# VectorE's order in a state space stage: tied to the source, with inputs and sums a step apart

## The chip, the core and the metric

One core of a Trainium2 chip runs a whole small network in one launch. The metric is the device time of that launch in microseconds. The engines are TensorE (PE, with its weight loads as PEld), VectorE (DVE), ScalarE (ACT), GpSimd (POOL) and SyncE (SP, which issues the DMAs). Each takes its instructions in the order in which they were queued; they meet through semaphores.

## The reference

Two blocks of two layers each work on 256 tokens of width 1024: projections, mixers, norms and MLPs, all in fp32. The change lies in the first mixer of the second block, `mixer_sb_ssm`. It projects the tokens to q, k, v and u, 512 wide each, and computes two things side by side.

Stick-breaking attention, 8 heads of 64: `z = q k / 8`; the weight of position s for query t is `sigmoid(z)` times the product of `1 - sigmoid(z)` over the positions after s and before t. So it needs log sums of `softplus(z)` along s, then an exponential, then the product with v.

A state space model, 32 groups of 64 complex states, 16 channels each: `x_t = a x_(t-1) + B u_t`, `y_t = Re(C x_t) + d u_t`, over the 256 tokens. After it come `y = gelu(y)`, a gate `y * sigmoid(y W + b)` (GLU) and the mixer's output projection.

## The kernel before, in words

All large matmuls run as three matmuls of split operands: a weight tile arrives by DMA (`raw`), ScalarE writes its rounded part (`hi`, L362), VectorE the rest (`lo`, L364), and TensorE forms hi*hi + hi*lo + lo*hi (`mm3`, L386 to L388). I call L362 and L364 a split. Weights come in a fixed sequence; a split is traced one or two units ahead of its use.

The work is traced by generators. The projections are the main line (`transposed`, `natural`), which yield every few matmuls; at each yield `step()` advances the side generators by one step each. A planner then orders the instructions of each engine: it goes through them by their place in the trace and its own estimates of time, and gives a tile its buffer from a pool of fixed size when the tile is first written. An instruction traced later can so be queued earlier. `behind(ins)` makes what is traced inside it follow `ins` on the same engine, without a semaphore.

`_ssm_run` is one side generator (from the u projection on), `side_attention` the other (from the first half of k and q on). The states fill 16 sets of 128 partitions, taken 4 at a time (q = 0 to 3) as tile k = 0 to 3. Tokens are taken in pairs, so that 128 steps of two tokens are left. For each k and q: two matmuls with K = 64 (L1883; in fp32 a matmul stands as two instructions in the trace) form the input in a PSUM bank, the row half depending on q % 2; VectorE rotates it by a phase (products with cos and sin, L1887 and L1888, sums L1889 and L1890, into `w`), and runs two scans along the steps (L1892, into `xs`). After four q the result is rotated back (L1902 to L1909, four products and two sums on 128x512), over `w`. `outputs` (L1850 to L1858) multiplies `w` by C on TensorE, one k later, and adds d*u on VectorE (L1860, into `yT`). A k has three steps: q = 0, 1; q = 2, 3; rotation.

The attention takes half a head pair per step s = 0 to 7: `stage_a` forms masked scores in a PSUM bank (L1323 to L1326), ScalarE makes |z|, exp, ln(1 + .) of them (L1329 to L1331), VectorE the softplus (L1332); `stage_b`, a step later, adds the triangular sums to the same bank (L1337 to L1341) and ScalarE takes the exponential (L1344); `stage_c` multiplies by v (L1352), whose tile `vn` ScalarE copies from PSUM (L1394).

Pools that matter: `b4` has 7 buffers (uT, yT, qT, kT, vn, up, each k's w and xs, and the two row loads of the next norm, L1529), `b2` has 12 (the attention's tiles, the rotation's four), `b1` 7, and the PSUM pool `psw` 4 banks (inputs of a q, scores, outputs, stage c). After the side work come the rows of the output projection (`_rows`), GELU (L1658 to L1663) and the GLU's matmuls.

Of the kernel before, what the change touches and what calls it, by code (L numbers as in the profile page):

```python
# [12 lines left out]
ALU = mybir.AluOpType  # L13
# [92 lines left out]
def _offsets():  # L106
    off, table = 0, {}
    for key, parts in _units().items():
        if key[0] == "up":
            nkt, ncol = sum(len(p[2]) for p in parts) // 128, len(parts[0][3])  # L110
        else:
            nkt, ncol = len(parts[0][2]) // 128, sum(len(p[3]) for p in parts)
        table[key] = (off, nkt, ncol)
        off += nkt * 128 * ncol
    return table, off
# [144 lines left out]
class _Env:  # L260
# [5 lines left out]
    def __init__(self, ctx, tc, ws):  # L266
        self.tc, self.nc, self.ws = tc, tc.nc, ws
        self.pools = {}
        self.ctx = ctx
        self.ps = {k: ctx.enter_context(tc.tile_pool(name="ps" + k, bufs=4, space=PSUM)) for k in "aw"}  # L270
        self.table, _ = _offsets()
        self.seq = _sequence()
        self.pos = {k: n for n, k in enumerate(self.seq)}
        self.raws, self.parts = {}, {}
        self.loaded = self.cut = 0
        self.n = 0
        self.side = []
        self.after = self.marks = ()
# [181 lines left out]
def _hilo(e, hi, lo, src):  # L460

    return (e.nc.scalar.activation(out=hi, in_=src, func=AF.Copy),
            e.nc.vector.tensor_tensor(out=lo, in0=src, in1=hi.bitcast(F32), op=ALU.subtract))


class _Act:
# [27 lines left out]
class _Norm(_Act):  # L494
# [8 lines left out]
    def slice(self, xT, c):  # L503
        self.add(xT[:, 2 * c:2 * c + 2], self.g[:, 2 * c:2 * c + 2])
        if c == 0:
            self.e.after = self.last
        self.square(xT, c)
# [48 lines left out]
def kernel(ctx: ExitStack, tc: tile.TileContext, x: bass.AP, p: bass.AP, prm1: bass.AP,  # L556
# [61 lines left out]
    for i in range(2):  # L618
# [44 lines left out]
        def load_emb(i=i):  # L663
            pt = e.t("b2", [128, 2, 256])
            nc.sync.dma_start(out=pt, in_=p[i])
            emb.extend(e.t("b2", [128, 2, 256], F32R) for _ in range(2))
            _hilo(e, *emb, pt)
# [53 lines left out]
        norm = nxt  # L721
        dump(f"xp{i}", xT)
    _second(e, K, xT, norm, ssm, ln, out, dump)


# [562 lines left out]
def _second(e, K, xT, act, S, ln, out, dump):  # L1288
    nc, tc = e.nc, e.tc
    V, A, G, PE = nc.vector, nc.scalar, nc.gpsimd, nc.tensor  # L1290
    P, C, ident, negones = S["P"], S["C"], K["ident"], K["negones"]
# [6 lines left out]
    uT = e.t("b4", [128, 4, 256])  # L1298
    for c in range(2):
        e.run(e.transposed(("su", c), act,  # L1300
                           lambda b, bank, c=c: A.activation(out=uT[:, 2 * c:2 * c + 2], in_=bank, func=AF.Copy)))
    e.drain_all()
    yT = e.t("b4", [128, 4, 256])
    run = _ssm_run(e, P, C, S, uT, yT)
    e.add(run)

    qT = e.t("b4", [128, 4, 256])
# [8 lines left out]
    sc, ws = {}, {}  # L1316

    def stage_a(s):
        j, g = s // 2, s % 2
        hs = slice(64 * g, 64 * g + 64)  # L1320
        ps = e.bank()
        diag = ps[:, :].rearrange("p (a q) -> p a q", a=4)[:, 0:4:2]
        PE.matmul(out=diag, lhsT=im[:, 0], rhs=smask2, start=True, stop=False, skip_group_check=True)  # L1323
        PE.matmul(out=ps[:, 0:256], lhsT=kT[hs, j, 0:128], rhs=qT[hs, j, :], start=False, stop=False,
                  skip_group_check=True)
        PE.matmul(out=ps[:, 256:384], lhsT=kT[hs, j, 128:256], rhs=qT[hs, j, 128:256], start=False, stop=False,  # L1326
                  skip_group_check=True)
        l = e.t("b2", [128, 384])
        A.activation(out=l, in_=ps[:, :384], func=AF.Abs)  # L1329
        A.activation(out=l, in_=l, func=AF.Exp, scale=-1.0)  # L1330
        A.activation(out=l, in_=l, func=AF.Ln, bias=1.0)  # L1331
        V.scalar_tensor_tensor(out=l, in0=ps[:, :384], scalar=0.0, in1=l, op0=ALU.max, op1=ALU.add)  # L1332
        sc[s] = (ps, l)

    def stage_b(s):
        ps, sp = sc.pop(s)
# [24 lines left out]
    def side_attention():  # L1361
        ready, lag = [], 1
        for s in range(8 + lag):
            while s >= 4 and "qk" not in D:
                yield
            if s < 8:
                stage_a(s)
            if s >= lag:
                stage_b(s - lag)
                if (s - lag) % 2:  # L1370
                    ready.append((s - lag) // 2)
            yield
            if ready and "v" in D:
                stage_c(ready.pop(0))
        while ready:
            yield
            stage_c(ready.pop(0))
# [461 lines left out]
    S.update(cos=cosE, sin=sinE, m=m2, bT=bT, cexp=cexp, k0=k0)  # L1839


def _ssm_run(e, P, C, S, uT, yT):

    nc = e.nc
    V, A, G, PE = nc.vector, nc.scalar, nc.gpsimd, nc.tensor

    def outputs(k, w):
        u = uT[:, k].rearrange("p (j r) -> p r j", r=2)
        y = e.bank()[:, :256].rearrange("p (r j) -> p r j", r=2)
        PE.matmul(out=y[:, 0], lhsT=S["k0"][:, k], rhs=u[:, 0], start=True, stop=False, skip_group_check=True)  # L1850
        for v, r, c in ((0, 1, 0), (1, 1, 1), (2, 0, 0), (3, 0, 1)):
            for q in range(4):
                h = slice(32 * q, 32 * q + 32)
                if r == 1:
                    PE.matmul(out=y[h, 1], lhsT=S["cexp"][:, v, 4 * k + q], rhs=w[:, q, c], start=False, stop=False,
                              skip_group_check=True)
                else:
                    PE.matmul(out=y[h, 0, 1:128], lhsT=S["cexp"][:, v, 4 * k + q], rhs=w[:, q, c, 0:127],  # L1858
                              start=False, stop=v == 3, skip_group_check=True)
        V.scalar_tensor_tensor(out=yT[:, k].rearrange("p (j r) -> p r j", r=2), in0=u, scalar=P["d"][:, k:k + 1],  # L1860
                               in1=y, op0=ALU.mult, op1=ALU.add)


    up = e.t("b4", [128, 4, 2, 128])
    for q in range(4):
        for r in range(2):
            o = 64 * (q % 2) + 32 * r
            src = uT[32 * q:32 * q + 32].rearrange("p k (j r) -> p r k j", r=2)[:, r]
            if r:
                G.tensor_copy(out=up[o:o + 32, :, q // 2], in_=src)  # L1870
            else:
                A.activation(out=up[o:o + 32, :, q // 2], in_=src, func=AF.Copy)
    yield
    prev = None
    for k in range(4):
        w = e.t("b4", [128, 4, 2, 128])
        xs = e.t("b4", [128, 4, 2, 128])
        s = slice(4 * k, 4 * k + 4)
        for q in range(4):
            h = slice(64 * (q % 2), 64 * (q % 2) + 64)  # L1880
            ps = e.bank()[:, :256].rearrange("p (c j) -> p c j", c=2)
            for c in range(2):
                PE.matmul(out=ps[:, c], lhsT=S["bT"][h, c, 2 * k + q // 2], rhs=up[h, k, q // 2])  # L1883
            st = 4 * k + q
            tc_ = e.t("b1", [128, 2, 128])
            ts_ = e.t("b1", [128, 2, 128])
            V.tensor_tensor(out=tc_, in0=ps, in1=S["cos"][:, st].unsqueeze(1).to_broadcast([128, 2, 128]), op=ALU.mult)  # L1887
            V.tensor_tensor(out=ts_, in0=ps, in1=S["sin"][:, st].unsqueeze(1).to_broadcast([128, 2, 128]), op=ALU.mult)  # L1888
            V.tensor_tensor(out=w[:, q, 0], in0=tc_[:, 0], in1=ts_[:, 1], op=ALU.add)  # L1889
            V.tensor_tensor(out=w[:, q, 1], in0=tc_[:, 1], in1=ts_[:, 0], op=ALU.subtract)  # L1890
            for c in range(2):
                V.tensor_tensor_scan(out=xs[:, q, c], data0=S["m"][:, st:st + 1].to_broadcast([128, 128]), data1=w[:, q, c], initial=0.0,  # L1892
                                     op0=ALU.mult, op1=ALU.add)
            if q % 2:
                yield
        if prev is not None:
            outputs(*prev)
        cosb = S["cos"][:, s]
        sinb = S["sin"][:, s]
        ta = e.t("b2", [128, 4, 128])  # L1900
        tb = e.t("b2", [128, 4, 128])
        V.tensor_tensor(out=ta, in0=xs[:, :, 0], in1=cosb, op=ALU.mult)  # L1902
        V.tensor_tensor(out=tb, in0=xs[:, :, 1], in1=sinb, op=ALU.mult)
        V.tensor_tensor(out=w[:, :, 0], in0=ta, in1=tb, op=ALU.subtract)
        tc2 = e.t("b2", [128, 4, 128])
        td = e.t("b2", [128, 4, 128])
        V.tensor_tensor(out=tc2, in0=xs[:, :, 1], in1=cosb, op=ALU.mult)
        V.tensor_tensor(out=td, in0=xs[:, :, 0], in1=sinb, op=ALU.mult)
        V.tensor_tensor(out=w[:, :, 1], in0=tc2, in1=td, op=ALU.add)  # L1909
        prev = (k, w)  # L1910
        yield
    outputs(*prev)
# [181 lines left out]
```

## Time and profile before

| | us |
|---|---|
| median of 3 runs (range) | 1472.47 (1470.43 to 1473.62) |
| the profiled execution | 1469.84 |
| its span | 1468.1 |
| TensorE, VectorE, ScalarE busy in the span | 1446.8, 1077.4, 779.8 |
| TensorE's mean granted clock, share of full speed | 0.993 |

A row of the timeline gives the start in us from the span's start, the length, the engine, the line, the operation, the tile written and the tiles read, and in brackets how long the engine stood idle before it and what ended that. Neighbouring rows can overlap: an engine starts an instruction before the last one has ended. A line of the list of waits reads: who waited, for whom, us in total, times, the longest. Busy time counts matmuls whose ends are modelled. [...]

### The profile page before, as it was taken

The numbers are of one execution on the slowest core, as the hardware profiler recorded it, in microseconds if no ns is written. First come the engines' busy times: TensorE is split into PE (matmuls) and PEld (weight loads), VectorE is DVE, ScalarE is ACT, GpSimd is POOL, SyncE is SP. The second block draws the span as 40 slices with busy tenths as digits, with TensorE's granted clock in tenths as the row PEclk, the third lists the DMA queues.
The fourth block names the chain that finished last, engine by engine and source line by source line (L and its number), as shares of the span: only waits on it lengthen the run. The fifth ranks groups of instructions, "written<-read, shape, count | busy, mean of one in ns | idle before, by whom it ended". The sixth has DMA issues, their size and how long they took to land.

```text
span 1468.1 us, 24862 instructions
## 1 busy us (share of the span) xinstructions
PE 1446.8 (99%) x9740; PEld 1282.8 (87%) x9740; DVE 1077.4 (73%) x1857; ACT 779.8 (53%) x1248; POOL 202.4 (14%) x142
## 2 busy tenths in 40 slices
PE   9999999999999999999999999999999999999997
PEld 7878999999998779999999998778888798788886
DVE  6786668666678796679877778868666788686666
ACT  6665445444557564454654555455545456654442
POOL 2343313000033333203000200000000100100000
PEclk9999999999999999999999999899999999999999
DMA  8552445555545553555555454235555452265551
GB/s 294 189 188 99 171 172 175 198 187 186 180 154 189 197 174 131 175 174 176 187 199 180 158 178 152 78 129 194 194 190 182 151 193 103 100 214 189 187 191 68
DMA packets 70677, 250.59 MB, mean 171 GB/s; under 512 B 8096, under 2 KB 8480, under 8 KB 70560
## 3 DMA queue, kind: packets, MB, share of 16 engines
q1 hardware_dynamic: 70560, 249.01, 49.6%
q8 instruction: 76, 1.25, 0.3%
q14 instruction: 41, 0.34, 0.1%
HBM read 247.93 MB, written 1.05 MB: 170 GB/s over the span
## 4 chain that ended last, share of the span: by engine, by line
PE 88%; DVE 6%; ACT 2%; DMA 2%; issue 1%; POOL 0%; DVEq 0%; SPq 0%; ACTq 0%; POOLq 0%
PE psa L386 16%; PE psa L387 16%; PE psa L388 16%; PE psw L436 15%; PE psw L438 8%; PE psw L386 3%; PE psw L387 3%; PE psw L388 3%; DMA raw<-in_ws_dram 2%; DVE lo L364 2%; PE psw L1076 1%; ACT hi L362 1%; PE psw L1883 1%; PE psw L2028 0%; PE psw L773 0%
## 5 line engine op out<-in xcount | busy, mean ns | idle before, releaser
L364 DVE TENSOR_TENSOR lo<-raw,hi 128x1024 fp32r<-128x1024 f32 (+1 forms) x416 | 515.3, 1245 | 224.7 <-ACT hi L362 223.4
L362 ACT ACTIVATE hi<-raw 128x1024 fp32r<-128x1024 f32 (+1 forms) x448 | 465.6, 1047 | 395.4 <-issue 153.7
L436 PE MATMUL psw<-act,hi 128*128 128x512 f32 x960 | 340.8, 397 | 0.0
L438 PE MATMUL psw<-act,lo 128*128 128x256 f32 x960 | 268.0, 281 | 0.0
L436 PEld LDWEIGHTS psw<-act,hi 128*128 128x128 f32 x960 | 179.9, 188 | 41.1
L438 PEld LDWEIGHTS psw<-act,lo 128*128 128x128 f32 x960 | 181.4, 189 | 1.7
L388 PE MATMUL psa<-b,lo 128*128 128x256 f32 x640 | 180.4, 283 | 0.0
L387 PE MATMUL psa<-b,hi 128*128 128x256 f32 x640 | 180.2, 283 | 0.0
L386 PE MATMUL psa<-b,hi 128*128 128x256 f32 x640 | 177.8, 283 | 0.0
L386 PE MATMUL psa<-act,hi 128*128 128x256 f32 x456 | 132.1, 291 | 0.0
L388 PE MATMUL psa<-act,lo 128*128 128x256 f32 x456 | 130.0, 286 | 0.8 <-DVE lo L364 0.8
L387 PE MATMUL psa<-act,hi 128*128 128x256 f32 x456 | 130.6, 287 | 0.0
L386 PE MATMUL psa<-hi,act 128*128 128x512 f32 (+2 forms) x320 | 122.7, 390 | 1.2 <-ACT act L481 0.4
L388 PEld LDWEIGHTS psa<-b,lo 128*128 128x128 f32 x640 | 122.0, 191 | 0.1
L387 PEld LDWEIGHTS psa<-b,hi 128*128 128x128 f32 x640 | 122.0, 191 | 0.0
L387 PE MATMUL psa<-lo,act 128*128 128x512 f32 (+2 forms) x320 | 121.1, 382 | 0.6 <-DVE lo L364 0.5
L386 PEld LDWEIGHTS psa<-b,hi 128*128 128x128 f32 x640 | 120.4, 190 | 1.2
L388 PE MATMUL psa<-hi,act 128*128 128x512 f32 (+2 forms) x320 | 116.8, 382 | 0.0
L386 PE MATMUL psa<-hi,b 128*128 128x512 f32 x256 | 99.6, 390 | 0.0
L387 PE MATMUL psa<-lo,b 128*128 128x512 f32 x256 | 99.6, 390 | 0.0
L364 POOL TENSOR_TENSOR lo<-raw,hi 128x1024 fp32r<-128x1024 f32 x32 | 77.5, 2423 | 157.1 <-ACT hi L362 140.0
L388 PE MATMUL psa<-hi,b 128*128 128x512 f32 x256 | 98.7, 389 | 0.0
(364 smaller groups left out, 2656.3 us busy)
## 6 DMA issues: line engine op xcount, KB each, us to landing
raw<-in_ws_dram SPq DMA_DIRECT2D x450, 512.0 KB, 4.0
b<-in_ln_dram SPq DMA_DIRECT2D x8, 512.0 KB, 4.9
raw<-in_ws_dram SPq DMA_DIRECT2D x8, 280.0 KB, 4.2
raw<-in_ws_dram SPq DMA_DIRECT2D x4, 264.0 KB, 2.5
b<-in_x_dram SPq DMA_DIRECT2D x4, 256.0 KB, 4.7
out_dram<-b SPq DMA_DIRECT2D x4, 256.0 KB, 2.0
cb<-in_cb_dram SPq DMA_DIRECT2D x1, 676.0 KB, 6.6
b<-in_p_dram SPq DMA_DIRECT2D x2, 256.0 KB, 5.6
```

What stands on the lines that cost most here:

```text
L362: self.nc.scalar.activation(out=hi, in_=w, func=AF.Copy)
L364: eng.tensor_tensor(out=lo, in0=w, in1=hi.bitcast(F32), op=ALU.subtract)
L386: mm(out=out, lhsT=lh, rhs=rh, start=start, stop=False, skip_group_check=shared)
L387: mm(out=out, lhsT=lh, rhs=rl, start=False, stop=False, skip_group_check=shared)
L388: self.mlast = mm(out=out, lhsT=ll, rhs=rh, start=False, stop=stop, skip_group_check=shared)
L436: mm(out=bank.rearrange("p (v t) -> p v t", v=2), lhsT=h[:, c], rhs=act[2][k], start=k == 0, stop=False, skip_group_check=True)
L438: mm(out=bank[:, :256], lhsT=l[:, c], rhs=act[0][k], start=False, stop=k == len(hi) - 1, skip_group_check=True)
L1076: PE.matmul(out=o[64 * gg:64 * gg + 64, q0:256], lhsT=kvn[:, kt, v0:v0 + 64], rhs=pts[s - 2 + 2 * gg][:, 256 * kt:256 * kt + 256 - q0], st ...
L1883: PE.matmul(out=ps[:, c], lhsT=S["bT"][h, c, 2 * k + q // 2], rhs=up[h, k, q // 2])
```

## The change

A class `_Chain` stands for VectorE in `_ssm_run` and for the softplus. Each instruction issued through it is put behind the one issued through it before, so that these instructions have the source's order on VectorE; others, the splits among them, may go between. The softplus moves out of `stage_a` to the start of the attention's next step. In `_ssm_run` a tile's eight input matmuls are issued together, one step ahead of VectorE's work on them, into two whole PSUM banks: bank n holds q = n and n + 2, which use the same half of the rows. VectorE then works on two q at once: products of 128x512 and sums of 128x256 in place of 128x256 and 128x128, with temporaries from `b2` in place of `b1`. The scans and the rotation keep their sizes. A k still has three steps: matmuls; products, sums and scans; outputs of the last k and rotation.

```diff
             e.nc.vector.tensor_tensor(out=lo, in0=src, in1=hi.bitcast(F32), op=ALU.subtract))
 
 
+class _Chain:
+
+
+    def __init__(self, e, engine):
+        self.e, self.engine, self.last = e, engine, ()
+
+    def __getattr__(self, name):
+        def call(**kw):
+            with self.e.behind(self.last):
+                ins = getattr(self.engine, name)(**kw)
+            self.last = (ins,)
+            return ins
+        return call
+
+
 class _Act:
 
 
@@ -1301,7 +1316,8 @@
                            lambda b, bank, c=c: A.activation(out=uT[:, 2 * c:2 * c + 2], in_=bank, func=AF.Copy)))
     e.drain_all()
     yT = e.t("b4", [128, 4, 256])
-    run = _ssm_run(e, P, C, S, uT, yT)
+    order = _Chain(e, V)
+    run = _ssm_run(e, P, C, S, uT, yT, order)
     e.add(run)
 
     qT = e.t("b4", [128, 4, 256])
@@ -1329,8 +1345,11 @@
         A.activation(out=l, in_=ps[:, :384], func=AF.Abs)
         A.activation(out=l, in_=l, func=AF.Exp, scale=-1.0)
         A.activation(out=l, in_=l, func=AF.Ln, bias=1.0)
-        V.scalar_tensor_tensor(out=l, in0=ps[:, :384], scalar=0.0, in1=l, op0=ALU.max, op1=ALU.add)
         sc[s] = (ps, l)
+
+    def softplus(s):
+        ps, l = sc[s]
+        order.scalar_tensor_tensor(out=l, in0=ps[:, :384], scalar=0.0, in1=l, op0=ALU.max, op1=ALU.add)
 
     def stage_b(s):
         ps, sp = sc.pop(s)
@@ -1363,6 +1382,8 @@
         for s in range(8 + lag):
             while s >= 4 and "qk" not in D:
                 yield
+            if s >= lag:
+                softplus(s - lag)
             if s < 8:
                 stage_a(s)
             if s >= lag:
@@ -1839,10 +1860,10 @@
     S.update(cos=cosE, sin=sinE, m=m2, bT=bT, cexp=cexp, k0=k0)
 
 
-def _ssm_run(e, P, C, S, uT, yT):
+def _ssm_run(e, P, C, S, uT, yT, V):
 
     nc = e.nc
-    V, A, G, PE = nc.vector, nc.scalar, nc.gpsimd, nc.tensor
+    A, G, PE = nc.scalar, nc.gpsimd, nc.tensor
 
     def outputs(k, w):
         u = uT[:, k].rearrange("p (j r) -> p r j", r=2)
@@ -1876,23 +1897,27 @@
         w = e.t("b4", [128, 4, 2, 128])
         xs = e.t("b4", [128, 4, 2, 128])
         s = slice(4 * k, 4 * k + 4)
-        for q in range(4):
-            h = slice(64 * (q % 2), 64 * (q % 2) + 64)
-            ps = e.bank()[:, :256].rearrange("p (c j) -> p c j", c=2)
+        pss = [e.bank().rearrange("p (a c j) -> p a c j", a=2, c=2) for _ in range(2)]
+        for a in range(2):
             for c in range(2):
-                PE.matmul(out=ps[:, c], lhsT=S["bT"][h, c, 2 * k + q // 2], rhs=up[h, k, q // 2])
-            st = 4 * k + q
-            tc_ = e.t("b1", [128, 2, 128])
-            ts_ = e.t("b1", [128, 2, 128])
-            V.tensor_tensor(out=tc_, in0=ps, in1=S["cos"][:, st].unsqueeze(1).to_broadcast([128, 2, 128]), op=ALU.mult)
-            V.tensor_tensor(out=ts_, in0=ps, in1=S["sin"][:, st].unsqueeze(1).to_broadcast([128, 2, 128]), op=ALU.mult)
-            V.tensor_tensor(out=w[:, q, 0], in0=tc_[:, 0], in1=ts_[:, 1], op=ALU.add)
-            V.tensor_tensor(out=w[:, q, 1], in0=tc_[:, 1], in1=ts_[:, 0], op=ALU.subtract)
-            for c in range(2):
-                V.tensor_tensor_scan(out=xs[:, q, c], data0=S["m"][:, st:st + 1].to_broadcast([128, 128]), data1=w[:, q, c], initial=0.0,
-                                     op0=ALU.mult, op1=ALU.add)
-            if q % 2:
-                yield
+                for n in range(2):
+                    h = slice(64 * n, 64 * n + 64)
+                    PE.matmul(out=pss[n][:, a, c], lhsT=S["bT"][h, c, 2 * k + a], rhs=up[h, k, a])
+        yield
+        for n in range(2):
+            st = slice(4 * k + n, 4 * k + n + 3, 2)
+            tc_ = e.t("b2", [128, 2, 2, 128])
+            ts_ = e.t("b2", [128, 2, 2, 128])
+            bc = lambda t: t[:, st].unsqueeze(2).to_broadcast([128, 2, 2, 128])
+            V.tensor_tensor(out=tc_, in0=pss[n], in1=bc(S["cos"]), op=ALU.mult)
+            V.tensor_tensor(out=ts_, in0=pss[n], in1=bc(S["sin"]), op=ALU.mult)
+            V.tensor_tensor(out=w[:, n::2, 0], in0=tc_[:, :, 0], in1=ts_[:, :, 1], op=ALU.add)
+            V.tensor_tensor(out=w[:, n::2, 1], in0=tc_[:, :, 1], in1=ts_[:, :, 0], op=ALU.subtract)
+            for q in (n, n + 2):
+                for c in range(2):
+                    V.tensor_tensor_scan(out=xs[:, q, c], data0=S["m"][:, 4 * k + q:4 * k + q + 1].to_broadcast([128, 128]),
+                                         data1=w[:, q, c], initial=0.0, op0=ALU.mult, op1=ALU.add)
+        yield
         if prev is not None:
             outputs(*prev)
         cosb = S["cos"][:, s]
```

## Rows read from the trace of the kernel before

**Rows 1.** The page, parts 1 and 4: busy engines, and the chain that ended last.
```profile
PE 1446.8 (99%) x9740; PEld 1282.8 (87%) x9740; DVE 1077.4 (73%) x1857; ACT 779.8 (53%) x1248; POOL 202.4 (14%) x142
...
PE 88%; DVE 6%; ACT 2%; DMA 2%; issue 1%; POOL 0%; DVEq 0%; SPq 0%; ACTq 0%; POOLq 0%
```

**Rows 2.** Windows: length, busy time (x instructions) of PE, PEld, DVE, ACT, POOL; PEclk; DMA.
```profile
887.10:952.60 65.50, 62.97 (x450) 52.81 (x450) 59.30 (x142) 28.70 (x48) 0.00 (x0) 0.92 0.31 105
935.30:949.20 13.90, 11.37 (x68) 9.13 (x68) 13.90 (x39) 6.33 (x13) 0.00 (x0) 0.63 0.11 38
938.90:948.00 9.10, 7.91 (x33) 6.20 (x35) 9.10 (x29) 4.22 (x10) 0.00 (x0) 0.50 0.15 51
```

**Rows 3.** Waits of TensorE, 886.4 to 968.5: us in total, times, longest.
```profile
PE psw L1883 <- DVE b L1860: 1.3, 1, 1.3
PE psw L1883 <- DVE b L1888: 1.2, 1, 1.2
```

**Rows 4.** Waits of VectorE, 887.1 to 952.6.
```profile
DVE b L1887 <- PE psw L1883: 2.5, 3, 1.8
DVE b L1332 <- ACT b L1331: 2.1, 1, 2.1
```

**Rows 5.** Timeline of TensorE at two runs of input matmuls: start, us, line, operation.
```profile
890.95 0.28 PE L388 MATMUL psa<-act,lo 128*128 128x256 f32 x1
891.07 0.28 PE L386 MATMUL psa<-act,hi 128*128 128x256 f32 x1
891.28 0.71 PE L1883 MATMUL psw<-b,b 64*128 64x128 f32 x4
...
892.14 0.28 PE L388 MATMUL psa<-act,lo 128*128 128x256 f32 x1
...
899.48 0.72 PE L1883 MATMUL psw<-b,b 64*128 64x128 f32 x8
```

**Rows 6.** Timeline of VectorE: starts of neighbouring products, sums and rotations.
```profile
890.22 0.42 DVE L1887 TENSOR_TENSOR b<-psw,b 128x256 f32<-128x256 f32 x1
890.55 0.41 DVE L1888 TENSOR_TENSOR b<-psw,b 128x256 f32<-128x256 f32 x1
...
903.10 0.68 DVE L1902 TENSOR_TENSOR b<-b,b 128x512 f32<-128x512 f32 x1
903.70 0.69 DVE L1903 TENSOR_TENSOR b<-b,b 128x512 f32<-128x512 f32 x1
...
929.97 0.41 DVE L1888 TENSOR_TENSOR b<-psw,b 128x256 f32<-128x256 f32 x1
930.41 0.29 DVE L1889 TENSOR_TENSOR b<-b,b 128x128 f32<-128x128 f32 x1
930.62 0.28 DVE L1890 TENSOR_TENSOR b<-b,b 128x128 f32<-128x128 f32 x1
```

**Rows 7.** Timeline of three engines: who waits for a buffer of b4.
```profile
920.65 0.29 DVE L1889 TENSOR_TENSOR b<-b,b 128x128 f32<-128x128 f32 x1
...
930.68 0.50 PE L1850 MATMUL psw<-b,b 128*128 128x128 f32 x2
...
932.44 0.62 PE L1858 MATMUL psw<-b,b 128*32 128x127 f32 x16
...
933.50 2.62 DVE L1892 TENSOR_TENSOR_SCAN b<-m,b 128x128 f32<-128x128 f32 x8
...
945.39 1.08 ACT L1394 ACTIVATE b<-psa 128x512 f32<-128x512 f32 x2 [1.30 <-PE psw L1326]
```

**Rows 8.** Timeline at the end of the stage: last rotation, outputs, GELU, GLU's matmuls.
```profile
951.95 0.68 DVE L1909 TENSOR_TENSOR b<-b,b 128x512 f32<-128x512 f32 x1
...
957.12 0.48 DVE L1860 SCALAR_TENSOR_TENSOR b<-b,prm,psw 128x256 f32<-128x256 f32 x1 [1.80 <-PE psw L1858]
...
965.58 1.23 DVE L463 TENSOR_TENSOR b<-b,b 128x1024 fp32r<-128x1024 f32 x1
...
968.49 0.41 PE L386 MATMUL psw<-b,hi 128*128 128x256 f32 x2
```

## The prediction, made before the change was run

> **What bounds the kernel now.** I read the page first: TensorE is busy for 99% of the span and makes up 88% of the chain that ended last, VectorE 6% [rows 1]. So a change of VectorE's order pays only where TensorE lost time to VectorE. I then cut the stage of the state space run into windows. Over 887.1 to 952.6 VectorE was busy for 59.30 of 65.50 us, so it idled 6.2. Over 935.3 to 949.2 TensorE idled 13.90 - 11.37 = 2.5 us, and from 938.9 to 948.0 its granted clock was 0.50, the lower of its two levels [rows 2]. TensorE's list of waits has just two, both for VectorE, 1.3 and 1.2 us, both ahead of L1883 [rows 3]. Those rows are the finding: from about 935 to 949 VectorE sets the pace, and before and after that TensorE runs without a gap. VectorE's own waits in the same stretch are 2.5 us for L1883's matmuls and 2.1 us for a softplus's ScalarE input [rows 4]; the remaining 1.6 us are short ones, mostly for weight splits.
>
> The stage ends like this: VectorE's last rotation is issued at 951.95 (0.68 us), the last outputs at 957.12, the GELU's last operand at 965.58 (1.23 us, so 966.8), and TensorE takes it up at 968.49 [rows 8]. Two things thus meet at 968.49: TensorE's filling work, without a gap since 949, and the GELU, ready 1.7 us before.
>
> **The change, part by part.** Input matmuls. There are 64 instructions before and after. Before, they came as 12 runs of 4 and 2 runs of 8. One run of 4 pushes the dense matmuls apart by 892.14 - 891.07 less two spacings of 0.12 (891.07 - 890.95): 0.83 us. A run of 8, on both halves of the rows, takes 0.72 us against 0.71 [rows 5]: the second half rides along. So before: 14 x 0.83 = 11.6 us. After, a tile has one run of 16, two such pairs back to back. No row shows a run of 16; between 0.83 (all rides along) and 0.83 + 0.65 I take 1.3, so 4 x 1.3 = 5.2 us, and TensorE has 6.4 us less to do.
>
> Fewer, longer VectorE instructions. The 32 products of 128x256 come 0.33 us apart (890.22 to 890.55); 128x512 comes 0.60 apart (903.10 to 903.70), read from SBUF, the nearest row. 16 x (0.66 - 0.60) = 1.0 us less; 0 if PSUM costs more at that size. The 32 sums of 128x128 come 0.21 apart (930.41 to 930.62) and become 16 of 128x256, which I price as the products' 0.33: 16 x (0.42 - 0.33) = 1.4. Together 0 to 2.4, taken as 2.0. The 32 scans stay as they are.
>
> [...]
>
> The tie to the source's order. It adds no semaphore, only an order on VectorE: each product, sum, scan, rotation, output and softplus behind the one traced before it. The splits (L364) stay free to go between. The price is that needing neighbours stand together: L1889 right behind the L1888 that it reads starts 930.41 - 929.97 = 0.44 us after it, not 0.33 [rows 6]. Four such pairs a tile (product to sum, twice; the rotation's two sums), so 16 x 0.11 = 1.8 us more, or 0 where a split falls between.
>
> Waits that go. A tile's matmuls are traced a step before its products, so VectorE's 2.5 us for L1883 should go. The softplus is traced a step behind its scores, so ScalarE's three passes lie beside a whole step of VectorE work, and the 2.1 us should go [rows 4]. That is 4.6 us. Both times a split or a scan that was ready stood behind the waiting instruction.
>
> A wait that comes. The pool b4 has 7 buffers. From tile 1 on uT, qT, kT, up, yT, w and xs hold all 7. The next tile's w takes the old xs once that is rotated, but its own xs has to wait for the old w, which the outputs read last. The trace shows it: tile 2's first sum is at 920.65, its scans only at 933.50, right behind L1858's outputs of tile 1 (932.44 + 0.62), the last reader of tile 1's w; and the value tile's copy (L1394) waited for L1326, the last reader of kT, until 945.39 [rows 7]. In the tied order tile 2's scans stand in the line: the softplus and the rotation stand behind them, and so does any split queued after them, for which TensorE's dense matmuls wait. The scans wait for the outputs of tile 1, and these for one of the 4 PSUM banks of their pool. That pool is freer than before (two banks a tile where four were taken). A bank comes free when the tile's first two products are read, 1.2 us into its VectorE work (2 x 0.60); the outputs took 2.4 us with a stage b between them (930.68 to 933.06), about 1.4 by estimate without; the scans are due at 2.0 (two products and two sums). So the stall is 0.6 to 1.6 us and some way on TensorE's queue, taken as 2.0. Tile 1 is spared, for one buffer is still free then, and tile 3, since up comes free once its matmuls are done. The bounds are 0 and 11 (rival B). The products' move from pool b1 to b2 I cost at nothing: a rotation needs two b2 buffers at a time in the source's order. No DMA is moved; the norm's two row loads on SP's queue wait for b4 too, and get it sooner.
>
> Sum for VectorE: -2.0 + 1.8 - 4.6 + 2.0 = -2.8 us for the end of the last rotation. From there to L1860 it took 957.12 - 952.63 = 4.5 us, of which the outputs' own matmuls are some 1.4; TensorE had stage c and rows between them. With its queue 6.4 us lighter I take 1.7 of the 3.1 back (0 to 3.1). The GELU starts 4.5 us earlier, and its slack of 1.7 at the end can be used too if TensorE is there: 6.2. TensorE's side allows it: 2.5 idle, half of the 8 us or so worked at half clock (4.0) and 6.4 make 12.9. So the later of the two is the GELU, and the matmuls at 968.49 move forward by 6.2 us. After them everything hangs on these, and the weights for it are cut before they are needed, so the 6.2 us stay. Profiled execution: span 1468.1, with what lies around it 1469.84; less 6.2 it is 1463.6. The median of the three runs is 2.6 above the profiled one, so I forecast 1466.3 us.
>
> **Rivals.** A: TensorE runs dry earlier and its clock falls for longer. For: it has 12.9 us to gain and VectorE lets it have 6.2, so some 6.7 us of idle must stand between about 923 and 947, while 2.5 us of it were followed by 9 us at the lower clock [rows 2]. Each us of work done at half clock costs another; 4.0 were lost before. If 10 are, 6 more go and the gain is gone: 1472. Against: stage c and the rows can fill the gaps, once the value tile is copied, and L1326's last reading comes earlier in the new order. [...]
>
> B: the new wait grows to what the trace has now. Tile 2's scans came 933.50 - 920.65 = 12.9 us after its first sum [rows 7], during which VectorE did other work; tied, it could do none of the line's. Less the 2 us of products and sums in between that is a stall of 11, 9 above what I took, so 2.8 later than now, and TensorE, without splits, would spend more of it at the lower clock: some 3 more, 1478. It decides from a stall of 2.0 + 6.2 = 8.2 us on. Against: the outputs were late because nothing asked for them.
>
> C: the open terms all go the good way: merged instructions 0.4 more, splits between the needing neighbours 1.8, no stall at the scans 2.0, the outputs right behind the rotation 1.4. That is 5.6 more, 11.8 in all, still under TensorE's 12.9: 1461.
>
> D: the planner puts most of the line where it was, and the tie does little: 1472, no change.
>
> **How the numbers follow.** Forecast 0.60 (0.57 of it faster), A 0.15, B 0.13, C 0.07, D 0.05. A measurement of this kernel can't tell a change of under 0.2%, 2.9 us, from none, so faster is below 1469.5: 0.57 + 0.07 = 0.64; the same 0.03 + 0.15 + 0.05 = 0.23; slower 0.13. The same four terms can go the other way by 2.0, 0, 2.0 (a stall of 4) and 1.7; they will not all go one way, so the forecast's own range is 1462 to 1470. For 8 in 10 it reaches to C's 1461 and over A and D, which end at 1472, to 1474; most of B is left out.
>
> **What would show it.** the input matmuls in 4 runs of 16; VectorE's waits for it and for the softplus gone; VectorE's last rotation 3 us earlier against the first product; TensorE's clock at 0.50 for no more than 9 us; the matmuls on the GELU's output some 6 us earlier, and the time from them to the end unchanged. I am wrong if VectorE stands still for over 8 us ahead of a scan, if the low clock lasts over 14 us, or if what follows the GELU takes the gain back.

## The result, and the profile after

The changed kernel takes 1485.53 us (median of 4 runs, 1484.24 to 1487.20) where the kernel before took 1472.08 on the same chip (1470.43 to 1473.62, 4 runs): 1.0092 times as long, with an interval of 1.0075 to 1.011. Faster was forecast, at 1466.3. The profiled execution took 1487.20, with a span of 1485.4.

Line numbers move: the input matmuls are L1905 now (L1883 before), the outputs' matmuls L1871, L1876 and L1879 (L1850 to L1858), the scores' matmuls L1339 to L1342, the exp L1363, the copy of v L1415 (L1394). The triangular sums are L1356 to L1360. All tied operations of VectorE, which I call the line, stand under L475, the helper. L462 and L463 split a computed tile (stage c's result, the GELU's) as L362 and L364 split a weight. All starts are 2.36 us later from the copies of u on, ahead of the changed part, which is a difference between two executions; shifts below are given less this.

The page of the kernel after, parts 1 and 4, against [rows 1]:

```profile
PE 1451.5 (98%) x9740; PEld 1286.5 (87%) x9740; DVE 1075.3 (72%) x1825; ACT 779.7 (52%) x1248; POOL 201.1 (14%) x142
...
PE 86%; DVE 7%; DMA 3%; ACT 2%; issue 2%; POOL 0%; DVEq 0%; SPq 0%; ACTq 0%; POOLq 0%
```

VectorE has 32 instructions fewer, as forecast. Windows of the kernel after: the two that answer to [rows 2], and a wider one. The third number from the end of such a row (PEclk) is the clock that TensorE was granted, as a share of full speed.

```profile
889.50:955.00 65.50, 59.07 (x392) 50.84 (x391) 47.86 (x88) 25.03 (x41) 0.00 (x0) 0.87 0.28 90
937.70:951.60 13.90, 11.28 (x45) 9.86 (x46) 11.76 (x26) 2.89 (x6) 0.00 (x0) 0.50 0.01 1
...
880.00:1000.00 120.00, 107.19 (x715) 89.60 (x714) 80.19 (x140) 52.49 (x82) 3.05 (x4) 0.90 0.30 97
```

The wide window of the kernel before:

```profile
880.00:1000.00 120.00, 115.91 (x800) 96.53 (x800) 94.89 (x197) 64.37 (x104) 7.30 (x10) 0.96 0.36 120
```

In the same 65.50 us VectorE now does 47.86 us of work instead of 59.30: it stands still for 17.6 us, not 6.2. TensorE idles 12.8 us in the wide window instead of 4.1, and its clock is 0.90 instead of 0.96. In stretches of 1 us the clock of both traces is 1.00 or 0.50, with values between only where it changes, so 0.90 over the window is 24 us at 0.50, and 0.96 is 9.6. Matmuls in a row start 0.21 us apart at 0.50 where they start 0.12 apart at 1.00 (the GLU's, kernel after, 985.06 to 988.90 and 989.53 to 992.04), and the last triangular sums start 0.42 after those before them instead of 0.22 (kernel before, 942.51 and 913.04). By these, if TensorE was at work in all of the 14.4 us more, they cost 0.44 to 0.48 of themselves: 6.3 to 6.9 us. With 8.7 of idle that is 15.0 to 15.6, an estimate. The next stage's first matmul, before and after, came 15.5 us later, which lies in that range and is near the profiled execution's whole loss of 15.0 (17.36 less 2.36):

```profile
996.71 0.63 PE L436 MATMUL psw<-act,hi 128*128 128x512 f32 x2
...
1014.60 0.63 PE L436 MATMUL psw<-act,hi 128*128 128x512 f32 x2
```

So the loss is all in this stage. VectorE's waits over 887 to 980 (us in total, times, longest) say for what:

```profile
DVE lo L364 <- ACT hi L362: 12.9, 8, 3.1
DVE b L475 <- PE psw L1342: 6.8, 1, 6.8
DVE b L475 <- PE psw L1879: 5.8, 2, 5.4
```

Both waits of the line are new. [Rows 4] had none longer than 2.1. The timeline of the kernel after shows where they stand, and who was late:

```profile
888.87 0.71 PE L1905 MATMUL psw<-b,b 64*128 64x128 f32 x4
891.25 0.71 PE L1905 MATMUL psw<-b,b 64*128 64x128 f32 x4
893.64 0.71 PE L1905 MATMUL psw<-b,b 64*128 64x128 f32 x4
894.66 1.28 DVE L475 TENSOR_TENSOR b<-psw,b 128x512 f32<-128x512 f32 x2
...
896.98 1.16 PE L1905 MATMUL psw<-b,b 64*128 64x128 f32 x16
...
921.20 1.23 DVE L364 TENSOR_TENSOR lo<-raw,hi 128x1024 fp32r<-128x1024 f32 x1 [1.47 <-ACT hi L362]
923.91 1.23 DVE L364 TENSOR_TENSOR lo<-raw,hi 128x1024 fp32r<-128x1024 f32 x1 [1.49 <-ACT hi L362]
924.26 1.16 PE L1905 MATMUL psw<-b,b 64*128 64x128 f32 x8
925.06 3.94 DVE L475 TENSOR_TENSOR b<-b,b 128x512 f32<-128x512 f32 x6
926.66 1.16 PE L1905 MATMUL psw<-b,b 64*128 64x128 f32 x8
...
931.16 0.76 DVE L475 TENSOR_TENSOR b<-b,b 128x256 f32<-128x256 f32 x2
933.47 0.39 PE L1339 MATMUL psw<-b 128*128 128x256 f32 x1 [0.96 <-ACT b L1363]
934.63 0.80 PE L1871 MATMUL psw<-b,b 128*128 128x128 f32 x2
936.21 1.07 PE L1879 MATMUL psw<-b,b 128*32 128x127 f32 x16
937.35 1.37 DVE L475 TENSOR_TENSOR_SCAN b<-m,b 128x128 f32<-128x128 f32 x4 [5.44 <-PE psw L1879]
...
944.48 3.09 PE L1905 MATMUL psw<-b,b 64*128 64x128 f32 x16
946.48 1.06 ACT L1415 ACTIVATE b<-psa 128x512 f32<-128x512 f32 x2
948.93 0.76 DVE L475 TENSOR_TENSOR b<-b,b 128x256 f32<-128x256 f32 x2
956.08 0.38 PE L1342 MATMUL psw<-b,b 64*128 64x128 f32 x2
956.50 1.37 DVE L475 TENSOR_TENSOR_SCAN b<-m,b 128x128 f32<-128x128 f32 x4 [6.81 <-PE psw L1342]
```

Four losses can be read from it. First, the first bank holds quarters 0 and 2, so the first product needs three of the four groups of matmuls, which come 2.4 us apart: it starts at 894.66, by 5.05 us later than before (887.25). Second, two splits that wait for ScalarE stand ahead of tile 1's rotation (925.06): 3.0 us. Third, tile 2's scans wait 5.44 us for the outputs of tile 1, which stand on TensorE's queue behind two sums and two scores; the second of these waits 0.96 us for the exp (933.47), which has to empty a bank. Fourth, tile 3's scans wait 6.81 us for the last reader of q and k: the copy of v took a buffer at 946.48, so no other was left. Together 20.3 us, of which 12.9 reach the last rotation, below. Tile 1's 16 input matmuls (896.98) are one run of 1.16 us; tile 2's came as two runs of 8, and tile 3's took 3.09 us (944.48), at a clock of 0.50.

The end of the stage, against [rows 8]:

```profile
967.22 0.68 DVE L475 TENSOR_TENSOR b<-b,b 128x512 f32<-128x512 f32 x1
...
974.31 0.48 DVE L475 SCALAR_TENSOR_TENSOR b<-b,prm,psw 128x256 f32<-128x256 f32 x1 [0.33 <-PE psw L1879]
...
982.73 0.79 PE L386 MATMUL psw<-b,hi 128*128 128x256 f32 x2 [2.59 <-ACT b L462]
983.20 1.22 DVE L463 TENSOR_TENSOR b<-b,b 128x1024 fp32r<-128x1024 f32 x1
```

The last rotation is 12.9 us late, and the GLU's first matmuls 11.9 us. Before, TensorE came to them without a gap; now it waits 2.59 us for the GELU. The same matmuls then start over 9.32 us instead of 5.65, at a clock of 0.65 (a window of the kernel after):

```profile
982.70:992.10 9.40, 8.42 (x48) 8.13 (x49) 3.06 (x6) 2.36 (x5) 0.00 (x0) 0.65 0.35 113
```

So of the 15.5 us some 11.9 were lost up to the GLU, and 3.7 in it.

### The profile page after: what moved, and what is told of

It is laid out like the page before. It is cut to its first block, busy times and chain, and to the rows that moved or that the text cites. A ratio compares the mean times of both kernels' runs of the same rounds, so it can differ in the third digit from the quotient of the medians.

```text
span 1485.4 us, 24819 instructions
## 1 busy us (share of the span) xinstructions
PE 1451.5 (98%) x9740; PEld 1286.5 (87%) x9740; DVE 1075.3 (72%) x1825; ACT 779.7 (52%) x1248; POOL 201.1 (14%) x142
## 4 chain that ended last, share of the span: by engine, by line
PE 86%; DVE 7%; DMA 3%; ACT 2%; issue 2%; POOL 0%; DVEq 0%; SPq 0%; ACTq 0%; POOLq 0%
PE psa L386 15%; PE psw L436 15%; PE psa L388 15%; PE psa L387 15%; PE psw L438 8%; PE psw L387 3%; PE psw L386 3%; PE psw L388 3%; DMA raw<-in_ws_dram 2%; DVE lo L364 2%; ACT hi L362 1%; PE psw L1091 1%; DVE b L475 1%; PE psw L2053 0%; PE psw L1073 0%
## 5 line engine op out<-in xcount | busy, mean ns | idle before, releaser
L364 DVE TENSOR_TENSOR lo<-raw,hi 128x1024 fp32r<-128x1024 f32 (+1 forms) x416 | 515.2, 1245 | 234.1 <-ACT hi L362 232.7
L362 ACT ACTIVATE hi<-raw 128x1024 fp32r<-128x1024 f32 (+1 forms) x448 | 465.6, 1047 | 401.6 <-issue 154.7
L364 POOL TENSOR_TENSOR lo<-raw,hi 128x1024 fp32r<-128x1024 f32 x32 | 77.5, 2421 | 160.7 <-ACT hi L362 148.7
```

Source lines behind the costliest of these rows:

```text
L362: self.nc.scalar.activation(out=hi, in_=w, func=AF.Copy)
L364: eng.tensor_tensor(out=lo, in0=w, in1=hi.bitcast(F32), op=ALU.subtract)
```

## Experiments

Each ratio is to the kernel before, timed on the same chip. Theory 1: the tie puts VectorE's work in one line, and the line stops where it needs something that TensorE's queue brings late, while VectorE has other work; the two banks add a late start.

**The parts by themselves: e1, e15, e16.** e1 is the kernel after without the tie, e15 the kernel before with the softplus a step later, e16 the kernel before with the inputs a step ahead in two banks and the wide operations that read them.

```diff
# e1, in the kernel after
-    order = _Chain(e, V)
+    order = V
# e15, in the kernel before
+            if s >= lag:
+                softplus(s - lag)
             if s < 8:
                 stage_a(s)
# e16, in the kernel before: the new layout of _ssm_run's products, no tie
+        pss = [e.bank().rearrange("p (a c j) -> p a c j", a=2, c=2) for _ in range(2)]
```

> The changed kernel with the tie alone taken out (order = V): the two-bank inputs and the softplus a step later stay. Theory 1 (the line): the loss is VectorE standing still at the head of the tied line, 5.4 us ahead of tile 2's scans and 6.8 us ahead of tile 3's, both for a buffer of b4, and 3.0 us behind splits. Without the tie the planner puts other work there, so these waits fall to under 3 us together; the late first product (5.0 us) stays; 1473 to 1478 us. Theory 2 (the layout): the loss is the two-bank layout, whose first product waits for three of four groups of matmuls and whose matmuls TensorE takes in another order; the tie is innocent; 1482 to 1487 us.

> The kernel before with one part of the change: VectorE's softplus of a score stands a step later in the source, ahead of the next score's stage, and nothing else. Forecast's step: the 2.1 us that VectorE waited for ScalarE's Ln (rows 4) go, on a path that ends late: 1469 to 1470.5. Rival (VectorE had other work while the Ln ran, and TensorE's order is that of the kernel before): no change, 1471 to 1472.

> The kernel before with the other part: a tile's inputs in two banks a step early, in wide operations; no tie, softplus where it was. Theory 1 (the late start of the first product is what e1_no_tie lost; the step of the sums did nothing): 1475 to 1477, as e1. Rival (the step of the sums cost part of it): 1471 to 1474.

e1: 1476.09, 1.0033 [1.0021, 1.0046]. e15: 1471.31, 0.9996 [0.9987, 1.0005]. e16: 1477.08, 1.0031 [1.0022, 1.0039]. So the later step of the softplus is worth nothing by itself, the inputs' new form costs some 5 us (e16 is 0.1 above theory 1's range), and the tie on top of it the other 9 of 13.5. In e15 VectorE's wait for ScalarE is still there, in the list of its waits:

```profile
DVE b L1336 <- ACT b L1331: 2.1, 1, 2.1
```

In e1 the line's two long waits are gone; what is left between VectorE and TensorE is short, and TensorE loses its time ahead of the GLU. Its list of VectorE's and TensorE's waits:

```profile
DVE b L1881 <- PE psw L1879: 1.2, 1, 1.2
...
PE psw L386 <- ACT b L462: 6.4, 1, 6.4
```

**The late start: e5, e6.** No tie, and the first tile in the old form; e6 also with the buffers freed as in e3, below. In both the first tile has four steps where the kernel before and the kernel after have three, so what stands behind it is traced a step later.

```diff
+        if k == 0:
+            ...   (a bank for each quarter, as in the kernel before)
+        else:
             pss = [e.bank()...
```

> The kernel after without the tie (VectorE takes ready work, as before), and with the first tile's inputs as the kernel before has them: a bank for each quarter, so that VectorE can begin when the first of the four matmul groups is there; tiles 1 to 3 keep the two banks. Theory 1 (the late start of the first product is paid at the end, since VectorE has no idle time behind it to make it up): 1476.1 less most of the 5.05 us by which the first product came late, so 1470 to 1473. Rival (the late start is slack, and what e1_no_tie has above the kernel before comes from the wide operations or from the order of TensorE in the later tiles): 1475 to 1477. On the trace, by theory 1, the first product stands at 887 to 890 us and not at 897.

> As e5, and the copy of v and the normalization's sums taken off the pool of the scans' outputs (the edit of e3_b4_relief). Theory 1: the buffer chain is also there without the tie, though only some 1 us is lost by it, so 1469 to 1472, about 1 us under e5. Rival (without the tie VectorE finds other work while a scan waits for its buffer): the same as e5 within 1 us.

e5: 1473.40, 1.0014 [1.0005, 1.0024]: the first product is at 886.48, and 2.7 of e1's 4.9 us are back, 0.4 short of theory 1's range; whether the added step holds back the rest was not run. e6: 1470.71, 1.0002 [0.9993, 1.0011], another 2.7 where 1 was expected. Without the tie the whole loss can be undone.

**What the line waits for: e2, e3, e13, e9, e7.** All are tied. e2 issues a tile's outputs with the next tile's inputs, in the working banks. e3 takes the copy of v off the pool b4 and issues the next norm's two row loads, which need it too, behind the run. e13 only gives the outputs the accumulators' banks. e9 has these banks and e2's place, with the outputs' reader a step later. e7 is e9 with e3's edit.

```diff
# e2; e9 and e7 keep its result for the reader, a step later
+        outputs(*prev)        # ahead of the yield behind the input matmuls
# e13, e9, e7
-        y = e.bank()[:, :256]
+        y = e.bank("a")[:, :256]
# e3, e7
-    vn = e.t("b4", [128, 2, 512])
+    vn = e.t("act", [128, 2, 512])
-    norm = new(None, 0, 0)
     ...
     e.drain(run)
+    norm = new(None, 0, 0)
```

> The changed kernel with a tile's outputs traced one step earlier, with the next tile's matmuls, ahead of the next scores. Theory 1: tile 2's xs gets its buffer as soon as tile 1's outputs have run, so the 5.4 us ahead of tile 2's scans fall to under 2, tile 3's 6.8 stay; 1478 to 1482 us. Theory 2: nothing of the loss goes; 1484 to 1487 us.

> The changed kernel with two takers away from pool b4 while the state space run lasts: vn comes from the pool act, and the next norm's two row loads are traced after the run. Theory 1: tile 3's xs finds up's buffer, so its 6.8 us fall to under 2; tile 2's 5.4 stay, since seven buffers are still full then; 1477 to 1481 us. Theory 2: nothing of the loss goes; 1484 to 1487 us.

> The kernel after with one edit: the outputs write to the accumulators' banks (e.bank("a")) and stay where they are in the source. Theory 1 (the outputs of tile 1 came late, at 934.6, because they stood on TensorE's queue behind scores and sums that held the four working banks; with banks of their own the planner can place them when their inputs are ready): the wait of 5.4 us ahead of tile 2's scans goes, that of tile 3 (6.8, by the buffer that the copy of v took) stays, and 4 to 9 of the 14 us come back: 1476 to 1481. Rival (the place in the source counts, as the planner gives outputs their due time by it): 1483 to 1487.

> The kernel of e7 without the edit of e3_b4_relief: the line is tied, the outputs are issued with the next tile's inputs and go to the accumulators' banks, but the copy of v takes its place in the pool of the scans' outputs again. Theory 1 (two things were missing at the scans of the later tiles, a place on TensorE's queue for the outputs and a free buffer, and each costs by itself): the wait ahead of tile 3's scans is back at 4 to 7 us and the time lies 2 to 4 us above e7, at 1473 to 1476. Rival (the outputs' place was all of it, and the buffer was late only because the outputs were): within 1 us of e7, 1470 to 1472.

> The kernel after, with its tie, and with everything that its line was seen to wait for taken off TensorE's queue: the outputs of a tile are traced with the inputs of the next one and go to the accumulators' banks (two of these are free in this stretch), the operation of VectorE that reads them is traced a step later, and the edit of e3_b4_relief frees the buffers. Theory 1 (the tie costs what its line waits for: 5.4 and 6.8 us ahead of the scans of tiles 2 and 3, moved to the outputs in e2): the waits of over 2 us in the line behind the first tile go, and 8 to 11 of the 14 us come back, so 1475 to 1478. Rival (a line always finds something to wait for, since TensorE's queue runs through the scores in its own order): another wait of 4 to 9 us stands in the line, and the time stays at 1481 to 1486.

e2: 1487.34, 1.0114 [1.01, 1.0127], a miss: nothing comes back. The scans no longer wait, but the next in the line does, the reader of the outputs, for matmuls that got their bank only when an exp had emptied it. Timeline of e2:

```profile
952.93 0.49 PE L1871 MATMUL psw<-b,b 128*128 128x128 f32 x2 [0.58 <-ACT b L1363]
...
954.50 0.48 DVE L475 SCALAR_TENSOR_TENSOR b<-b,prm,psw 128x256 f32<-128x256 f32 x1 [8.69 <-PE psw L1879]
```

e3: 1483.10, 1.0082 [1.0069, 1.0096], 2.4 us back where 4.5 to 8.5 were expected. Tile 3's wait is gone, tile 2's is not; timeline of e3:

```profile
936.38 1.37 DVE L475 TENSOR_TENSOR_SCAN b<-m,b 128x128 f32<-128x128 f32 x4 [5.69 <-PE psw L1879]
```

So a freed buffer alone moves little, and an earlier place alone nothing. e13: 1476.03, 1.0026 [1.0015, 1.0038]: the banks alone bring 9.5 of the 13.5 us back. The outputs of tile 1 now run at 926.65 to 929.7, and the line's longest wait in 925 to 960 is 1.1 us for ScalarE. Theory 1 had tile 3's wait of 6.8 us stay, for the buffer; it is gone as well, so early outputs free a buffer too. TensorE comes to the GLU without a wait, so part of the 9.5 is the GLU's: its matmuls start over 5.64 us, as in the kernel before (5.65, at a clock of 1.00), against 9.32 in the kernel after (at 0.65). What remains in this stretch is three splits of stage c that wait for ScalarE. TensorE's timeline of e13, and VectorE's waits over 925 to 960:

```profile
926.65 0.43 PE L1876 MATMUL psa<-b,b 128*32 128x128 f32 x8
...
928.62 1.09 PE L1879 MATMUL psa<-b,b 128*32 128x127 f32 x16
...
DVE act L463 <- ACT act L462: 5.2, 3, 2.6
DVE b L475 <- ACT b L1347: 1.1, 1, 1.1
```

e9: 1474.24, 1.0014 [1.0005, 1.0023]. e7: 1471.35, 1.0013 [0.9996, 1.003]. The tied kernel is back at the time of the kernel before: all of the loss, where theory 1 had 8 to 11 us of it come back in e7. The medians of e9 and e7 differ by 2.9 us, inside theory 1's 2 to 4, the ratios do not (one of e7's ten runs took 1481.64), so that difference is open; and the wait that theory 1 expected in e9 ahead of tile 3's scans is not there (0.84 us), as its rival said. A late copy of v (at 938.24, in e7 at 924.4) makes stage c late instead, and its split stands in front of the last sums for 3.98 us. Timeline of e9:

```profile
940.91 1.37 DVE L475 TENSOR_TENSOR_SCAN b<-m,b 128x128 f32<-128x128 f32 x4 [0.84 <-PE psa L1879]
942.20 1.26 DVE L475 TENSOR_TENSOR b<-psw,b 128x512 f32<-128x512 f32 x2
947.44 0.42 DVE L463 TENSOR_TENSOR act<-psw,act 128x256 fp32r<-128x256 f32 x1 [3.98 <-ACT act L462]
947.78 0.75 DVE L475 TENSOR_TENSOR b<-b,b 128x256 f32<-128x256 f32 x2
```

VectorE's waits of e7 over 925 to 960, and its wide window:

```profile
DVE act L463 <- ACT act L462: 2.1, 2, 2.0
DVE b L475 <- PE psa L1879: 1.5, 1, 1.5
...
880.00:1000.00 120.00, 113.33 (x805) 94.48 (x804) 93.75 (x165) 64.87 (x104) 7.29 (x10) 0.99 0.34 116
```

No wait in the line is over 1.5 us, TensorE idles 6.7 us instead of 12.8, and the clock is 0.99.

**An earlier start in the freed line: e8, e10.** e8 is e7 with the first tile in the old form, e10 is e7 with the quarters of u copied in the order 0, 2, 1, 3.

```diff
# e10
-    for q in range(4):
+    for q in (0, 2, 1, 3):
```

> As e7, with the first tile's inputs as in the kernel before (the edit of e5). Theory 1: 4 to 5 us below e7, so 1470 to 1474, about the kernel before. Rival of the line that always waits: the 5 us that the line begins earlier are lost again at the next thing it waits for, so within 2 us of e7.

> The kernel of e7 with the four quarters of u copied in the order 0, 2, 1, 3, so that the first bank (quarters 0 and 2) is full after two copies instead of three. Theory 1 (the late start is the last part of what the change lost): the first product stands 2.4 us earlier against the copies, and the time falls by 1.5 to 2.5 us against e7, to 1469 to 1470. Rival (as in e8, where the line began earlier and the planner's order of TensorE turned it into waits): no gain or a loss, 1471 to 1476.

e8: 1479.47, 1.0056 [1.0039, 1.0073]; e10: 1473.32, 1.001 [0.9999, 1.002]. Both misses for theory 1, and e8 is outside of both expectations. In e10 the first product came 2.6 us earlier, less the difference of the starts, and the GELU 0.2 us earlier: 960.93 against 960.95, at starts 0.19 us apart the other way. The line, ahead of its time, met splits that were not ready. VectorE's timeline of e10:

```profile
918.00 1.23 DVE L364 TENSOR_TENSOR lo<-raw,hi 128x1024 fp32r<-128x1024 f32 x1 [2.66 <-ACT hi L362]
920.66 1.23 DVE L364 TENSOR_TENSOR lo<-raw,hi 128x1024 fp32r<-128x1024 f32 x1 [1.44 <-ACT hi L362]
```

In e8 splits that were not ready stood in the line as well, 2.06 us ahead of tile 1's scans, 2.81 ahead of its rotation, and 2.59 between the last tile's products and sums, where e7 has 1.96; TensorE then waited 4.51 us for the GELU. No one of these is the 8 us above e7, and e8's first tile has the added step of e5, so e8 does not show what an earlier start alone does. VectorE's timeline of e8:

```profile
951.04 0.42 DVE L463 TENSOR_TENSOR act<-psw,act 128x256 fp32r<-128x256 f32 x1 [2.59 <-ACT act L462]
...
952.03 0.75 DVE L475 TENSOR_TENSOR b<-b,b 128x256 f32<-128x256 f32 x2
```

So the 5.05 us of late start are not a loss that comes back by itself: an earlier start gave 2.7 us in e5, nothing in e10.

**Is there a gain to be had: e4, e12, e11, e14.** e4 is the kernel before with e3's edit, e12 that with the outputs in the accumulators' banks. e11 is e7 without the tie, e14 is e8 without it. Their edits are shown above.

> The kernel before with the same relief of pool b4 (vn from act, the norm's row loads after the run). Theory 1: the value tile is copied right after its matmuls, some 18 us earlier than 945.4, so stage c can fill TensorE's gaps between 935 and 949; tile 2's scans still wait for tile 1's outputs; 1467 to 1471 us. Theory 2 says nothing of it; if b4 doesn't matter in the kernel before, 1472.

> The kernel before, with its outputs in the accumulators' banks and the edit of e3_b4_relief: what cured the tied line, given to the kernel without the change. Theory 1 (the banks and buffers bind only where VectorE may not take other work): 1469 to 1472, no change. Rival (they hold up the kernel before as well, and e7's recovery is theirs and not the line's): 1463 to 1468.

> The kernel of e7 without the tie. Theory 1 (the tie costs only what its line waits for, and e7 has none of that left): within 1.5 us of e7, 1470 to 1473. Rival 1 (the tie, where nothing stops it, saves what VectorE loses by taking splits and scores between the steps of the run): 1473 to 1476. Rival 2 (the tie still costs, by splits that stand in the line): 1467 to 1470.

> No tie; first tile as in the kernel before; outputs issued with the next tile's inputs, to the accumulators' banks, and their reader a step later; the edit of e3_b4_relief. Theory 1 (all kernels that lost their waits come to the same end, since TensorE then stands idle ahead of the GLU and loses its clock, so that what is won in the state-space stage is paid there): 1469 to 1473, no change against the kernel before. Rival (5 us of start and 1 to 3 us of waits are real): 1464 to 1468, faster than the kernel before.

| kernel | us (median) | ratio | GLU's first matmul, less the start's difference | GLU, first to last start, us |
|---|---|---|---|---|
| before (profiled run) | 1472.08 | 1 | 968.49 | 5.65 |
| after | 1485.53 | 1.0092 [1.0075, 1.011] | 980.37 | 9.32 |
| e4 | 1471.00 | 1.0002 [0.9993, 1.0011] | 966.30 | 8.24 |
| e12 | 1471.88 | 1.0005 [0.9997, 1.0014] | 965.73 | 9.72 |
| e11 | 1471.60 | 1.0002 [0.9991, 1.0012] | 964.88 | 9.71 |
| e14 | 1472.86 | 1.0008 [1.0, 1.0017] | 967.77 | 8.05 |
| e6 | 1470.71 | 1.0002 [0.9993, 1.0011] | 965.80 | 8.25 |
| e7 | 1471.35 | 1.0013 [0.9996, 1.003] | 968.10 | 5.98 |

None is faster; e4 is at the upper end of its expectation, the other three are as theory 1 had them. e11 against e7: a tie whose waits are gone changes nothing that these runs can tell. The table shows where a gain goes. In five kernels TensorE is through with its other work sooner and starts the GLU 0.7 to 3.6 us earlier, but it has waited 2.3 to 4.5 us for the GELU's split, and the same matmuls then take 2.4 to 4.1 us longer. A wait and a window of e11:

```profile
PE psw L386 <- ACT b L462: 2.5, 1, 2.5
...
970.00:985.00 15.00, 14.62 (x76) 12.80 (x75) 7.39 (x16) 6.43 (x12) 0.55 (x1) 0.89 0.21 74
```

The granted clock is 0.89 there; in e7, where TensorE comes to the GLU without a wait (its last, 2.29 us for a split of stage c, ended at 966.86, 2.9 us ahead), it is 1.00 in the same window.

## Why the prediction was wrong

The sign was wrong. The failed step is the new wait: "The scans wait for the outputs of tile 1", "taken as 2.0", and "Tile 1 is spared, for one buffer is still free then, and tile 3, since up comes free once its matmuls are done." It measured 5.44 us at tile 2 and 6.81 at tile 3. The mechanism was named, and it is rival B's; two sentences of the argument were wrong. "the outputs were late because nothing asked for them" took the planner to move TensorE's work to what VectorE's line needs. It did not: the outputs stood behind two scores, and waited for their bank with them. e13 shows that this was the larger part: other banks alone give 9.5 us back. And at tile 3 the copy of v took one of the two buffers that were to be free. e3 bears this out: with the copy and the row loads out of the pool the wait is gone, and the row loads were issued only at 956.49 in the kernel after, behind the wait. Which buffer went to whom the traces do not show, and in e13 early outputs do away with the wait as well. Rival B's condition, a stall of over 8.2 us, was met, by 12.2 as the sum of two waits, but its 1478 was too low, since it had one wait and no late start.

Step by step:

- Input matmuls: a run of 16 was taken as 1.3 us. One lasts 1.16, and a run of 4 pushed the dense matmuls apart by 0.12 more than its length (0.83 against 0.71); that makes 1.28, as priced. But only tile 1 has such a run. The first tile keeps four runs of 4, tile 2 has two of 8 that take 1.16 each, and tile 3's 16 take 3.09 at a clock of 0.50: by their lengths 9.4 us, where 5.2 were priced. So most of the 6.4 us that TensorE was to have less to do did not come. And the first product waits for three of the first tile's four runs. These 5.05 us were not in the sum at all; e5 gives 2.7 of them back, e10 none.
- Merged instructions: two products take 1.28 us, two sums 0.76, which are 0.60 and 0.34 apart beside one length; forecast were 0.60 and 0.33. So the 2.0 us were priced about right, and they are lost in the waits.
- The tie: 1.8 us for needing neighbours was the small price. A larger one is that the splits, left free, are put between the line's operations in an order fixed ahead, so the line also waits for ScalarE: 3.0 us ahead of tile 1's rotation, 2.0 to 4.0 in e7 and e9 ahead of the last sums. The prediction had the splits wait for the line, not the line for the splits. It is not the tie's alone: in e1, without it, VectorE waits 3.07 and 1.07 us for two splits at 927.19 and 929.95.
- Waits that go: the 2.5 us for the input matmuls went. The 2.1 us for the softplus went in the kernel after, but e15 shows that the later step in the trace alone does not take it away. Whether any time hung on it no run shows.
- The end: 1.7 us were to come back between the last rotation and the GELU's input; it took 6.4 us instead of 4.5. The 1.7 us of slack ahead of the GLU were to be used as well; TensorE waits 2.59 there instead.
- "TensorE's side allows it: ... 12.9". This failed too, and more runs bear on it than on any other step. Its 4.0 took half of the 8 us at half clock; by the spacings above it is 0.44 to 0.48 of them, 3.5 to 3.8. TensorE's idle time and its half clock were no reserve to draw on here: e4, e6, e11, e12 and e14 began the GLU 0.7 to 3.6 us earlier and paid 2.4 to 4.1 in it. Of this 0.8 to 1.3 us is a second wait, for VectorE's split (L463); and over 970 to 985 the granted clock is 0.92 in e6, 0.89 in e11, 0.84 in e12 and 0.95 in e14, where e7 has 1.00. That is the lower clock of rival A at another place. At its own place it came as well: the window that had the clock at 0.63 has it at 0.50 from end to end, 13.9 us.

Of the signs named, the low clock of over 14 us came (24 us by the mean of the wide window); VectorE did not stand still for 8 us ahead of one scan, but for 12.2 ahead of two. There was no gain for what follows the GELU to take back, but it took 3.7 us more than before.

Open: whether e9 and e7 differ; what an earlier start is worth without the added step of e5 and e8; and how much the tie alone would cost the kernel before, which no run has: the 9 us are what it costs on top of the inputs' new form.

## What to carry to other kernels

An engine's work that is tied into one line must be priced by every foreign thing that the line takes up, with its place on the other engine's queue and the bank and the buffer that it needs first; what a free order hides behind ready work, a line pays in full. Find who holds each buffer at each step by listing all users of its pool, not only those of the change. And when the bound engine is at 99%, ask of a gain elsewhere what that engine will do in the time that comes free.

## What the runs showed of the hardware

The GLU's 48 matmul instructions started over 5.64 to 5.98 us in the six traces where TensorE came to them without a wait (before, e7, e9, e10, e13, e15), and over 8.05 to 9.72 us in the other twelve, behind a wait of 2.3 to 6.4 us; the granted clock over them was 1.00 in the kernel before and 0.65 in the kernel after. These matmuls started 0.12 us apart where the clock was 1.00 (kernel after, 989.53 to 992.04), and 0.21 apart where it was 0.50 (985.06 to 988.90). At a clock of 1.00, 16 input matmuls in pairs on both halves of the rows, the two of a pair 0.01 us apart, took 1.16 us (tile 1, 896.98), as long as 8 that came one by one (tile 2, 924.26); 8 in pairs took 0.72, as 4 one by one 0.71 [rows 5].
